# Two small row transfers in place of eight, and the last output product cut in three parts instead of four

## The chip, the cores and the metric

The kernel runs on one core of a Trainium2 chip. The metric is device time in microseconds (us) of one launch. The kernel before took 723.99 us (median of three runs, 723.14 to 724.71).

## The reference

One layer of a transformer-like block on 512 tokens of width 1024, in float32:

```
mod = silu(c) @ ada_w + ada_b;  sh1, sc1, g1, sh2, sc2, g2 = split(mod, 6)
h   = rmsnorm(x, norm1_g) * (1 + sc1) + sh1
xr, gr, u, v = split(h @ w_in, 4)
mix = concat(rg_lru(conv(xr)) * gelu(gr), spatial_gating(gelu(u), gelu(v))) @ w_out
x   = x + g1 * mix
h   = rmsnorm(x, norm2_g) * (1 + sc2) + sh2
y   = sum over each token's top-2 experts (of 32, chosen by group, then in the group):
          weight * ((silu(h @ w1[e]) * (h @ w3[e])) @ w2[e])
x   = x + g2 * y
out = rmsnorm(x, final_g)
```

All weights are read once: about 38 MB in front of the experts, 201 MB for the experts (6.3 MB each).

## The kernel before

**The front** (to about 242 us) is written out by hand in large part. SyncE issues nearly all transfers, in program order, from one queue. They use eight semaphores in turn, and a transfer is issued only when the eighth one before it has landed; a transfer into a buffer that was used before waits for the last reader as well. Transfers of 1 MB go round in five buffers (`w8`). `Ada.load` (L185 to 197) brings one unit of `ada_w` as two such buffers; `Ada.mm(kk)` (L199 to 211) is the product of one of the two halves with the condition. `Block` holds a quarter of `w_in`, split into a high and a low part by ScalarE and VectorE (L242, L244). `proj_step` (L440 to 446) is one eighth of a projection: 12 matmuls. The order on TensorE at the start is: transposes of x, `unit[0].mm(0)`, `unit[0].mm(1)`, `proj_step(b_xr, 0)`, `unit[1].mm(0)`, half of `proj_step(b_xr, 1)`, `unit[1].mm(1)`, the other half, and so on.

Between the loads of `unit[0]`, the first half of `b_xr` and those of `unit[1]`, SyncE issues the vectors that the second norm needs (norm2_g and two thirds of ada_b, L257 to 264): eight transfers into `rows_b`, each picking every fourth float of its source, so that one transpose of `rows_b` (L491) turns them, along with other vectors, into columns (`cols_b`, `cols_g`). The columns of `cols_g` are first read much later (`modulate2`).

**The experts** are worked off in 16 blocks of two or four experts, on 128 slots of tokens. Each block streams w1, w3 and w2 through a ring of twelve 1 MB buffers (`RING`, `slot8`), then computes `up(w1)`, `up(w3)`, the product with w2 (`mm`, L1161 to 1167) and adds the result to x2 by a product with a transposed one-hot matrix (`combine`).

**The last block** has four experts in column groups of 32. Its w2 product is cut by `LAST` in four parts of 256 output columns. Each part needs two buffers: a buffer holds two experts' four row chunks (two transfers of 512 KB, contiguous pieces of 1 KB). `y_part(i)` runs part i's product (four chunks q, four experts each) and scales it; all but the last are split into two parts for the combine. `combine_part(i)` adds part i to x2 for the four token tiles and sums squares on ScalarE; `scales` and `finish` apply the final norm and store. The order is y0, y1, combine 0, y2, combine 1, y3, combine 2, combine 3, then the four tiles' scaling and stores.

Of the kernel before, what the change touches and what calls it, by code (L numbers as in the profile page):

```python
# [7 lines left out]
F32 = mybir.dt.float32  # L8
# [4 lines left out]
OP = mybir.AluOpType  # L13
AX = mybir.AxisListType

P = 128
S, D, KD = 512, 1024, 8
NT = S // P
E, F, FC = 32, 512, 4
# [19 lines left out]
FIRST = ["wp"] * WP + ["wq"] * WQ + ["ft"] * 4 + ["l8"] * 3  # L39
WARM = 18  # L40
EPS = 1e-6
LAST = tuple((slice(c, c + 256), 4) for c in range(0, 1024, 256))


@with_exitstack
def trunk(ctx, tc, a, out):
    nc = tc.nc
    sync, act, pool, dve, pe = nc.sync, nc.scalar, nc.gpsimd, nc.vector, nc.tensor
# [10 lines left out]
    fa = mixer.enter_context(tc.tile_pool(name="fa", bufs=1, side="right"))  # L59
# [46 lines left out]
    off = {}  # L106
# [15 lines left out]
    rows_b = fa.tile([P, P], F32, name="rows_b")  # L122
# [11 lines left out]
    ident = const.tile([P, P], F32, name="ident")  # L134
# [30 lines left out]
    n = 0  # L165
# [88 lines left out]

    unit[0].load()
    b_xr.load(0)
    n = 40  # L257
    for name, ap in (("g2n", a["norm2_g"][0]), ("ada2", a["ada_b"][0, 3072:5120])):
        ap = ap.rearrange("(k c i) -> i k c", c=P, i=4)
        k = 4 * ap.shape[1]  # L260
        for i in range(4):
            sync.dma_start(rows_b[n + i:n + k:4], ap[i])  # L262
        off[name] = n - 40
        n += k
    unit[1].load()
    unit[2].load()
    b_xr.load(1)
# [222 lines left out]
    pt = bank("m", (P, P))  # L490
    pe.transpose(pt, rows_b, ident)  # L491
    dve.tensor_copy(cols_b, pt)
    dve.tensor_copy(cols_g, pt[:, 40:64])
    sw = [t2((P, 4, P)) for i in range(2)]
    for i in range(2):
        act.dma_start(sw[i], a["sgu_w"][0].rearrange("h i j -> i h j")[:, 4 * i:4 * i + 4, :])
# [542 lines left out]
    class Weights:  # L1039

        def __init__(self, name, b, f, cs=None, n=1):
            if b not in experts:
                experts[b] = []
                for e in range(BLOCKS[b][0], BLOCKS[b][0] + BLOCKS[b][1]):
                    if e >= FIXED:
                        e = nc.values_load(expert[0:1, e:e + 1], engines=[mybir.EngineType.SP], min_val=FIXED,
                                           max_val=E - 1)
                    experts[b].append(bass.ds(e, 1))  # L1050
            self.cs, self.f, self.n = cs, f, n
            if cs is None:
                self.src = [rows_of(a[name][0, e], f) for e in experts[b]]
            else:
                self.src = [a[name][0, e].rearrange("e (k p) f -> p (e k) f", p=P)[:, :, cs] for e in experts[b]]
            self.r = [[] for e in experts[b]]
            m = 1 if cs is None else 2
            self.todo = [(j, k) for k in range(0, self.src[0].shape[1], n) for j in range(0, len(self.src), m)]

        def load(self, most=2 * KD):  # L1060

            for q in range(min(most, len(self.todo))):
                j, k = self.todo.pop(0)
                if self.cs is None:
                    t = slot8((P, 2 * D))
                    sync.dma_start(t, self.src[j][:, k])
                    w = t.rearrange("p (i f) -> p i f", f=self.f)
                    self.r[j] += [w[:, q, :] for q in range(w.shape[1])]
                    continue
                t = slot8((P, 2, self.n, self.src[0].shape[2]))  # L1070
                for i in range(2):
                    sync.dma_start(t[:, i], self.src[j + i][:, k:k + self.n])  # L1072
                    self.r[j + i] += [t[:, i, q, :] for q in range(self.n)]

    def block_weights(b):
        if b == NB - 1:
            w2 = [Weights("expert_w2", b, D, cs, n) for cs, n in LAST]
        else:
            w2 = [Weights("expert_w2", b, D)]
        return Weights("expert_w1", b, F), Weights("expert_w3", b, F), w2  # L1080
# [9 lines left out]
    def block(b, along, early, before_y, after):  # L1090
# [67 lines left out]
                u()  # L1158
        yh, yl = yb[:, 0], yb[:, 1]

        def mm(ys, i=None):  # L1161
            for q in range(FC):
                for hf, y in enumerate(ys):
                    for c, n, j in cols:
                        w = w2[0][j][q][:, hf * F:(hf + 1) * F] if i is None else w2[i][j][q]
                        pe.matmul(y[c:c + n], gT[:, q, c:c + n], w,  # L1166
                                  start=(q == 0), stop=(q == FC - 1), tile_position=(0, c))
# [164 lines left out]
    tags = ["c", "m", "c", "m", "h"]  # L1332
    ncomb = [0]

    def y_part(i):

        cs = LAST[i][0]
        n = cs.stop - cs.start
        y = bank("y", (P, n))
        mm([y], i)  # L1340
        yf = t2((P, n))
        dve.tensor_tensor(yf, y, g2b[:, cs], op=OP.mult)
        if i == len(LAST) - 1:
            return ((cT.bitcast(F32), yf),)
        yh, yl = kept[0][:, 0, cs], kept[0][:, 1, cs]
        split(yh, yl, yf)
        return (cT, yh), (cT, yl)
# [2 lines left out]
    ms, base, both, v, r = [fin[:, n_parts - 1 + i] for i in range(5)]  # L1350

    def combine_part(i, parts):
        cs = LAST[i][0]
        n = cs.stop - cs.start
        for t in range(NT):
            ps = bank(tags[ncomb[0] % len(tags)], (P, n))
            ncomb[0] += 1
            for q, (w, y) in enumerate(parts):
                pe.matmul(ps, w[:, t, :], y, start=(q == 0), stop=(q == len(parts) - 1))
            xc = x2[:, t, cs]  # L1360
            dve.tensor_tensor(xc, xc, ps, op=OP.add)
            sq = t2((P, n))
            act.activation(sq, xc, AF.Square, scale=1.0 / 32.0, accum_out=fin[:, i, t:t + 1])
            if i < n_parts - 2:
                pool.tensor_tensor(xc, xc, fg[:, cs], op=OP.mult)
            tt = slice(t, t + 1)
            if i == n_parts - 1:
                dve.tensor_tensor(both[:, tt], base[:, tt], fin[:, i - 1, tt], op=OP.add)
                act.activation(r[:, tt], ms[:, tt], AF.Sqrt, bias=both[:, tt])
# [16 lines left out]
    todo = []  # L1386
    for i in range(n_parts):
        todo.append((i, y_part(i)))
        if 0 < i < n_parts - 1:
            combine_part(*todo.pop(0))  # L1390
    dve.scalar_tensor_tensor(base, fin[:, 0], EPS, fin[:, 1], op0=OP.add, op1=OP.add)
    for i, parts_ in todo:
        combine_part(i, parts_)
    for ts in (0, 1), (1, 3), (3, 4):
        scales(slice(*ts))
        for t in range(*ts):
# [24 lines left out]
```

## Time and profile before

| | |
|---|---|
| median of three runs | 723.99 us |
| profiled execution | 725.12 us, of which the span from the first to the last instruction is 723.3 us |
| TensorE busy | 658.3 us (91%) |
| VectorE, ScalarE, GpSimdE busy | 297.0, 178.1, 25.0 us |
| moved by DMA | 246.28 MB, mean 340 GB/s |
| mean granted TensorE clock | 0.962 |

In the profile, DMA engines are busy all the time from about 270 to 690 us (420 GB/s), and less in the front. In the rows, PE is TensorE, PEld its weight loads, DVE VectorE, ACT ScalarE, POOL GpSimdE, and SPq the issuing of transfers by SyncE. A busy share of DMA can be a little over 1 since it is worked out from packets' times.

### The profile page before, as it was taken

The page shows a single profiled execution, that of the slowest core. Times are in us where ns is not written, and L with a number is a line of the kernel's source. Part 1 is how long each engine was busy: PE and PEld are TensorE (multiplying, and loading weights), DVE is VectorE, ACT ScalarE, POOL GpSimd, SP SyncE. Part 2 cuts the span into 40 slices and gives each one's busy share as a digit, 9 for nine tenths or more (in the row PEclk, how much of TensorE's full clock was granted, in tenths as well). Part 3 has the DMA queues.
Part 4 walks back from the last instruction along what each step waited for, and adds up shares of the span by engine and source line. Part 5 has one row for each costly group of instructions (what it writes and reads, how often), then busy time and mean ns, then how long its engine had stood idle before and what let it go on. Part 6 is the DMA issues. An engine that isn't in the chain of part 4 may idle for free.

```text
span 723.3 us, 9703 instructions
## 1 busy us (share of the span) xinstructions
PE 658.3 (91%) x3693; PEld 358.2 (50%) x3693; DVE 297.0 (41%) x684; ACT 178.1 (25%) x317; POOL 25.0 (3%) x55
## 2 busy tenths in 40 slices
PE   7699999999998889987999999978799999998773
PEld 6356766777787444432444454513244445442132
DVE  7258638635468843321323333312132333224025
ACT  5135277532255121100101111000010111100114
POOL 3000001000103000000000000000000000000011
PEclk9799999999999999999999999989999999999887
DMA  8699902895528569999999999999999999999993
GB/s 295 200 346 305 318 24 97 271 367 183 218 124 316 218 255 427 400 422 420 421 423 420 420 419 422 420 421 419 423 421 420 420 422 420 421 421 421 383 335 120
DMA packets 68827, 246.28 MB, mean 340 GB/s; under 512 B 11064, under 2 KB 29096, under 8 KB 45224
## 3 DMA queue, kind: packets, MB, share of 16 engines
q1 hardware_dynamic: 67496, 245.08, 86.2%
q8 instruction: 30, 0.49, 0.3%
q10 hardware_dynamic: 1056, 0.52, 0.3%
q14 instruction: 21, 0.17, 0.1%
q0 software_dynamic: 224, 0.02, 0.0%
HBM read 243.51 MB, written 2.10 MB: 340 GB/s over the span
## 4 chain that ended last, share of the span: by engine, by line
PE 64%; DMA 21%; DVE 5%; ACT 4%; SPq 4%; issue 1%; POOL 0%; DVEq 0%; ACTq 0%
PE h L1119 21%; PE y L1166 11%; DMA w8r<-in_expert_w 10%; PE m L955 6%; DMA w<-in_expert_w 5%; PE c L969 4%; DMA l<-in_expert_w 4%; PE c L446 4%; PE h L446 3%; PE m L204 3%; PE y L446 2%; SPq L262 2%; DMA w<-in_ada_w 2%; SPq L1072 1%; PE h L90 1%
## 5 line engine op out<-in xcount | busy, mean ns | idle before, releaser
L1119 PE MATMUL h<-w,l 128*64 128x512 f32 (+1 forms) x616 | 152.5, 615 | 11.0 <-DMA w<-in_expert_w 11.0
L1119 PEld LDWEIGHTS h<-w,l 128*64 128x64 f32 (+1 forms) x616 | 42.8, 128 | 99.3 <-issue 76.6
L970 DVE TENSOR_TENSOR x<-x,c 128x512 f32<-128x512 f32 x96 | 65.8, 685 | 39.0 <-PE c L969 39.0
L1119 PE MATMUL h<-w8r,l 128*32 128x512 f32 (+1 forms) x304 | 69.8, 612 | 2.8 <-DMA w8r<-in_expert_w 2.8
L969 PE MATMUL c<-l,cT 128*128 128x512 f32 x192 | 62.6, 407 | 0.0
L1166 PE MATMUL y<-w8q,gT 128*64 128x512 f32 (+2 forms) x240 | 55.1, 626 | 5.2 <-DMA w8q<-in_expert_w 4.5
L1166 PE MATMUL y<-w8r,gT 128*64 128x512 f32 (+2 forms) x240 | 54.1, 611 | 5.5 <-DMA w8r<-in_expert_w 5.5
L955 PE MATMUL m<-l,b16h 128*128 128x256 f32 (+1 forms) x192 | 51.8, 294 | 3.1 <-ACT l L826 3.0
L994 DVE TENSOR_TENSOR t<-y,g2b 128x512 f32<-128x512 f32 x24 | 16.6, 691 | 92.3 <-PE y L1166 92.3
L1119 PE MATMUL h<-l,l 128*64 128x512 f32 (+1 forms) x120 | 52.5, 609 | 1.5 <-DMA l<-in_expert_w 1.5
L86 ACT ACTIVATE l<-t 128x512 fp32r<-128x512 f32 (+1 forms) x35 | 21.3, 612 | 128.5 <-DVE t L994 118.3
L1146 DVE SCALAR_TENSOR_TENSOR t<-t,ws,h 128x512 f32<-128x512 f32 x13 | 9.7, 747 | 97.2 <-PE h L1119 97.2
L955 PE MATMUL m<-l,b16l 128*128 128x256 f32 (+1 forms) x192 | 49.3, 281 | 0.0
L826 ACT ACTIVATE l<-m,s2c 128x256 f32<-128x256 f32 (+1 forms) x24 | 13.1, 546 | 146.2 <-PE m L955 146.2
L955 PEld LDWEIGHTS m<-l,b16h 128*128 128x128 f32 x192 | 36.3, 189 | 19.7 <-ACT l L826 8.3
L244 DVE TENSOR_TENSOR w8r<-w,w8r 128x512 fp32r<-128x512 f32 x48 | 30.6, 683 | 34.1 <-ACT w8r L242 34.1
L955 PEld LDWEIGHTS m<-l,b16l 128*128 128x128 f32 x192 | 36.3, 189 | 2.4
L1166 PEld LDWEIGHTS y<-w8r,gT 128*64 128x64 f32 (+1 forms) x240 | 15.4, 132 | 42.2 <-issue 30.0
L446 PE MATMUL c<-b16h,w8r 128*128 128x512 f32 x80 | 32.3, 427 | 4.2 <-ACT b16h L415 3.7
L242 ACT ACTIVATE w8r<-w 128x512 fp32r<-128x512 f32 x48 | 26.9, 621 | 33.1 <-PE h L92 14.1
L1119 PEld LDWEIGHTS h<-w8r,l 128*32 128x32 f32 (+1 forms) x304 | 17.8, 123 | 34.3 <-issue 28.9
L969 PEld LDWEIGHTS c<-l,cT 128*128 128x128 f32 x192 | 29.4, 189 | 6.7 <-DVE x L970 4.2
(359 smaller groups left out, 941.3 us busy)
## 6 DMA issues: line engine op xcount, KB each, us to landing
w<-in_expert_w SPq DMA_DIRECT2D x77, 1024.0 KB
w8r<-in_expert_w SPq DMA_DIRECT2D x60, 1024.0 KB
w8q<-in_expert_w SPq DMA_DIRECT2D x30, 1024.0 KB
l<-in_expert_w SPq DMA_DIRECT2D x17, 1024.0 KB
w<-in_ada_w SPq DMA_DIRECT2D x16, 1024.0 KB
w<-in_ada_w SPq DMA_DIRECT2D x16, 512.0 KB
w<-in_w_in SPq DMA_DIRECT2D x8, 1024.0 KB
w<-in_w_out SPq DMA_DIRECT2D x4, 1024.0 KB
```

Of the source, the lines that this page charges most:

```text
L86: act.activation(hi, src, AF.Copy)
L204: pe.matmul(self.ps[32 * j:32 * j + 32], cond[:, k:k + 1].to_broadcast([P, 32]), self.w[k // 4][:, j, :], start=(k < 4), stop=(k >= 4), ti ...
L242: act.activation(hi, raw, AF.Copy)
L244: return lambda: dve.tensor_tensor(lo, raw, hi.bitcast(F32), op=OP.subtract)
L262: sync.dma_start(rows_b[n + i:n + k:4], ap[i])
L446: pe.matmul(ps[c], lhs, rhs, start=(k == 0 and n == 0), stop=(k == KD - 1 and n == 2))
L955: pe.matmul(hold[k], src[:, t, chunk(k)], g[:, t, :], start=(t == 0 and i == 0), stop=(t == NT - 1 and i == 1))
L969: pe.matmul(ps, cT[:, t, :], y[:, cs], start=(i == 0), stop=(i == 1))
L970: dve.tensor_tensor(x2[:, t, cs], x2[:, t, cs], ps, op=OP.add)
L994: dve.tensor_tensor(yf, y, g2b[:, cs], op=OP.mult)
L1119: pe.matmul(h[c:c + n], xT[:, k, c:c + n], w[j][k], start=(k == 0), stop=(k == KD - 1), tile_position=(0, c))
L1166: pe.matmul(y[c:c + n], gT[:, q, c:c + n], w, start=(q == 0), stop=(q == FC - 1), tile_position=(0, c))
```

## The change

The second norm's vectors come as two transfers of whole rows into a small tile `rows_d` (six rows of 512 floats). Four transposes, each taking every fourth column of `rows_d`, make the columns, and one copy puts them in the same order as before into `cols_g`.

`LAST` is now one part of 512 columns and two of 256. A buffer holds the same row chunks of all four experts: one chunk for the half, two for a quarter. It is filled by four transfers of 256 KB (pieces of 2 KB for the half, of 1 KB for the quarters). `y_part` may be given something to run between its chunks 0 to 1 and 2 to 3: combine 0 stands amid the second part's product, combine 1 amid the third's; combine 2 ends the work.

```diff
-LAST = tuple((slice(c, c + 256), 4) for c in range(0, 1024, 256))
+LAST = (slice(0, 512), slice(512, 768), slice(768, 1024))
...
-    for name, ap in (("g2n", a["norm2_g"][0]), ("ada2", a["ada_b"][0, 3072:5120])):
-        ap = ap.rearrange("(k c i) -> i k c", c=P, i=4)
-        k = 4 * ap.shape[1]
-        for i in range(4):
-            sync.dma_start(rows_b[n + i:n + k:4], ap[i])
+    rows_d = fa.tile([6, 512], F32, name="rows_d")
+    sync.dma_start(rows_d[0:2], a["norm2_g"][0].rearrange("(k f) -> k f", f=512))
+    sync.dma_start(rows_d[2:6], a["ada_b"][0, 3072:5120].rearrange("(k f) -> k f", f=512))
...
-    dve.tensor_copy(cols_g, pt[:, 40:64])
+    pt = bank("m", (P, 4, 6))
+    for i in range(4):
+        pe.transpose(pt[:, i, :], rows_d.rearrange("r (c i) -> r i c", i=4)[:, i, :], ident[0:6, 0:6])
+    dve.tensor_copy(cols_g.rearrange("p (r i) -> p i r", i=4), pt)
...
+            self.n = n = 1 if cs is None else 2048 // (len(self.src) * (cs.stop - cs.start))
+            self.todo = [(j, k) for k in range(0, self.src[0].shape[1], n)
+                         for j in range(len(self.src) if cs is None else 1)]
...
-                t = slot8((P, 2, self.n, self.src[0].shape[2]))
-                for i in range(2):
-                    sync.dma_start(t[:, i], self.src[j + i][:, k:k + self.n])
+                t = slot8((P, len(self.src), self.n, self.src[0].shape[2]))
+                for j, s in enumerate(self.src):
+                    sync.dma_start(t[:, j], s[:, k:k + self.n])
...
+            mm([y], i, range(FC // 2))
+            between()
+            mm([y], i, range(FC // 2, FC))
...
+    part0 = y_part(0)
+    part1 = y_part(1, lambda: combine_part(0, part0))
+    def second_part():
+        combine_part(1, part1)
+        dve.tensor_scalar(base, fin[:, 0], EPS, None, op0=OP.add)
+    combine_part(2, y_part(2, second_part))
```

SyncE's queue at the start, as a piece of the difference (- before, + after); `w_155` is the first half of `b_xr`, `w_165` and `w_160` the first buffer of `unit[1]`:

```order
 L234 DMA w_155<-in_w_in 128x4x512
-L262 DMA rows_b<-in_norm_g 2x128x1 x4
-L262 DMA rows_b<-in_ada_b 4x128x1 x4
-L194 DMA w_165<-in_ada_w 128x4x256 x2
-L194 DMA w_168<-in_ada_w 128x4x256 x2
-L194 DMA w_171<-in_ada_w 128x4x256 x2
+L258 DMA rows_d<-in_norm_g 2x512
+L259 DMA rows_d<-in_ada_b 4x512
+L194 DMA w_160<-in_ada_w 128x4x256 x2
+L194 DMA w_163<-in_ada_w 128x4x256 x2
+L194 DMA w_166<-in_ada_w 128x4x256 x2
```

Two transfers stand now where eight stood, ahead of the same loads of `unit[1]`.

TensorE at the end of the program, before; y is the w2 product (L1166), `cT` the one-hot matrix of the combine, `t_5329` the last part's scaled result:

```order
L1166 MATMUL y<-w8r,gT 32x256 x16
L1359 MATMUL m<-l_2120,cT 128x256 x2
L1359 MATMUL h<-l_2120,cT 128x256 x2
L1359 MATMUL c<-l_2120,cT 128x256 x2
L1359 MATMUL m<-l_2120,cT 128x256 x2
L1359 MATMUL c<-t_5329,cT 128x256
L1359 MATMUL m<-t_5329,cT 128x256
L1359 MATMUL h<-t_5329,cT 128x256
L1359 MATMUL c<-t_5329,cT 128x256
```

Here all 16 matmuls of y's last part run first, and then the combines of the last two parts.

The same place after; the last part's result is `t_5321`:

```order
L1166 MATMUL y<-w8r,gT 32x256 x8
L1364 MATMUL h<-l_2120,cT 128x256 x2
L1364 MATMUL c<-l_2120,cT 128x256 x2
L1364 MATMUL m<-l_2120,cT 128x256 x2
L1364 MATMUL c<-l_2120,cT 128x256 x2
L1166 MATMUL y<-w8r,gT 32x256 x8
L1364 MATMUL m<-t_5321,cT 128x256
L1364 MATMUL h<-t_5321,cT 128x256
L1364 MATMUL c<-t_5321,cT 128x256
L1364 MATMUL m<-t_5321,cT 128x256
```

The eight matmuls of the last but one combine moved ahead of the last eight matmuls of y, and y's last part is cut in two groups of eight.

SyncE's last weight transfers after, with what each waits for (`DMAHW` is one of the eight semaphores of landed transfers; `w8_5046` and `w8_5051` are buffers of the half):

```order
L1072 DMA w8_5046<-in_expert_w2 128x512 [waits DMAHW6_49,PE_49]
L1072 ISA
L1072 DMA w8_5046<-in_expert_w2 128x512 [waits DMAHW7_49]
L1072 ISA
L1072 DMA w8_5046<-in_expert_w2 128x512 [waits DMAHW0_49]
L1072 ISA
L1072 DMA w8_5046<-in_expert_w2 128x512 [waits DMAHW1_49]
L1072 ISA
L1072 DMA w8_5051<-in_expert_w2 128x512 [waits DMAHW2_49,PE_49]
```

Each transfer is now half as large (the last block's w2 comes in 32 instead of 16), and there are still eight semaphores.

## Rows read from the trace of the kernel before

**Rows 1.** The page's clock and DMA lines, in 40 slices, in tenths

```profile
PEclk9799999999999999999999999989999999999887
DMA  8699902895528569999999999999999999999993
```

**Rows 2.** Chain of waits from 0 to 110 us: start, us, what

```profile
9.51 1.32 SPq L262
10.87 6.66 SPq L262
...
23.84 0.94 SPq L194
...
25.92 8.37 DMA w<-in_ada_w
34.34 1.11 PE m L204 x8
...
39.58 0.23 PE h L446
```

**Rows 3.** Windows of 2 us: busy by engine, clock, DMA share, GB/s

```profile
22.00:24.00 2.00, 2.00 (x6) 1.51 (x6) 1.11 (x2) 0.00 (x0) 0.00 (x0) 0.50 0.25 2
...
26.00:28.00 2.00, 0.19 (x1) 0.00 (x0) 0.00 (x0) 0.00 (x0) 0.00 (x0) 0.94 1.01 345
...
40.00:42.00 2.00, 2.00 (x8) 0.70 (x10) 1.48 (x3) 0.00 (x0) 0.00 (x0) 0.50 1.08 360
42.00:44.00 2.00, 2.00 (x16) 0.36 (x8) 0.00 (x0) 0.00 (x0) 0.00 (x0) 0.67 1.10 348
```

**Rows 4.** Timeline, TensorE around 26 us: start, us, instruction [idle before]

```profile
25.56 0.63 PE L446 MATMUL c<-b16l,w8r 128*128 128x512 f32 x1
29.65 1.94 PE L204 MATMUL m<-w,cond 128*32 128x512 f32 x8 [3.46 <-DMA w<-in_ada_w]
```

**Rows 5.** Chain of waits from 676 us on

```profile
687.00 8.40 DMA l<-in_expert_w
...
698.85 8.90 DMA w8r<-in_expert_w
...
707.79 1.93 PE y L1166 x26
...
717.70 0.72 ACT x L1381
```

**Rows 6.** Timeline, small operations like those that are added

```profile
2.26 0.24 PE L340 MATMUL m<-ident,rows_c 8*128 8x8 f32 x1 [2.26 <-DMA rows_c<-in_c]
3.45 0.32 SPq L114 DMA_DIRECT2D rows_a<-in_ada_b  x1
51.08 0.49 PE L446 MATMUL c<-b16h,w8r 128*128 128x512 f32 x1 [0.47 <-DVE w8r L244]
```

**Rows 7.** Chain of waits from 110 to 310 us

```profile
119.06 1.29 DVE w8r L244 x2
120.37 5.33 DMA w<-in_ada_w
...
307.46 15.05 DMA w<-in_expert_w
```

**Rows 8.** Timeline of the last block and the end

```profile
683.89 0.13 PEld L1119 LDWEIGHTS h<-w,l 128*32 128x32 f32 x1 [2.42 <-DMA w<-in_expert_w]
...
710.69 0.60 PE L1359 MATMUL c<-t,cT 128*128 128x256 f32 x2
...
712.31 0.40 ACT L1363 ACTIVATE t<-x 128x256 f32<-128x256 f32 x1
```

**Rows 9.** Windows of 10 and 2 us with different transfer shapes

```profile
140.00:150.00 10.00, 10.00 (x48) 7.95 (x50) 2.50 (x4) 2.20 (x4) 0.00 (x0) 1.00 1.04 384
...
698.00:700.00 2.00, 1.11 (x10) 0.49 (x8) 1.69 (x5) 1.18 (x6) 0.31 (x1) 1.00 1.10 350
...
718.00:720.00 2.00, 0.00 (x0) 0.00 (x0) 0.39 (x1) 0.42 (x1) 0.00 (x0) 0.50 1.02 380
```

More of the change, by code (lines that the diff above doesn't have):

```diff
@@ L256, in trunk @@
     b_xr.load(0)
-    n = 40
-    for name, ap in (("g2n", a["norm2_g"][0]), ("ada2", a["ada_b"][0, 3072:5120])):
-        ap = ap.rearrange("(k c i) -> i k c", c=P, i=4)
-        k = 4 * ap.shape[1]
-        for i in range(4):
-            sync.dma_start(rows_b[n + i:n + k:4], ap[i])
-        off[name] = n - 40
-        n += k
+    rows_d = fa.tile([6, 512], F32, name="rows_d")
+    sync.dma_start(rows_d[0:2], a["norm2_g"][0].rearrange("(k f) -> k f", f=512))
+    sync.dma_start(rows_d[2:6], a["ada_b"][0, 3072:5120].rearrange("(k f) -> k f", f=512))
+    off["g2n"], off["ada2"] = 0, 8
     unit[1].load()
@@ L1039, in trunk, with __init__ @@
     class Weights:
-        def __init__(self, name, b, f, cs=None, n=1):
+        def __init__(self, name, b, f, cs=None):
             if b not in experts:
@@ L1050, in __init__ @@
                     experts[b].append(bass.ds(e, 1))
-            self.cs, self.f, self.n = cs, f, n
+            self.cs, self.f = cs, f
             if cs is None:
@@ L1056, in __init__ @@
             self.r = [[] for e in experts[b]]
-            m = 1 if cs is None else 2
-            self.todo = [(j, k) for k in range(0, self.src[0].shape[1], n) for j in range(0, len(self.src), m)]
+            self.n = n = 1 if cs is None else 2048 // (len(self.src) * (cs.stop - cs.start))
+            self.todo = [(j, k) for k in range(0, self.src[0].shape[1], n)
+                         for j in range(len(self.src) if cs is None else 1)]
         def load(self, most=2 * KD):
@@ L1069, in load @@
                     continue
-                t = slot8((P, 2, self.n, self.src[0].shape[2]))
-                for i in range(2):
-                    sync.dma_start(t[:, i], self.src[j + i][:, k:k + self.n])
-                    self.r[j + i] += [t[:, i, q, :] for q in range(self.n)]
+                t = slot8((P, len(self.src), self.n, self.src[0].shape[2]))
+                for j, s in enumerate(self.src):
+                    sync.dma_start(t[:, j], s[:, k:k + self.n])
+                    self.r[j] += [t[:, j, q, :] for q in range(self.n)]
     def block_weights(b):
         if b == NB - 1:
-            w2 = [Weights("expert_w2", b, D, cs, n) for cs, n in LAST]
+            w2 = [Weights("expert_w2", b, D, cs) for cs in LAST]
         else:
@@ L1159, in block, with mm @@
         yh, yl = yb[:, 0], yb[:, 1]
-        def mm(ys, i=None):
-            for q in range(FC):
+        def mm(ys, i=None, qs=range(FC)):
+            for q in qs:
                 for hf, y in enumerate(ys):
@@ L1333, in trunk, with y_part @@
     ncomb = [0]
-    def y_part(i):
-        cs = LAST[i][0]
+    def y_part(i, between=None):
+        cs = LAST[i]
         n = cs.stop - cs.start
         y = bank("y", (P, n))
-        mm([y], i)
+        if between is None:
+            mm([y], i)
+        else:
+            mm([y], i, range(FC // 2))
+            between()
+            mm([y], i, range(FC // 2, FC))
         yf = t2((P, n))
@@ L1352, in combine_part @@
     def combine_part(i, parts):
-        cs = LAST[i][0]
+        cs = LAST[i]
         n = cs.stop - cs.start
@@ L1363, in combine_part @@
             act.activation(sq, xc, AF.Square, scale=1.0 / 32.0, accum_out=fin[:, i, t:t + 1])
-            if i < n_parts - 2:
+            if i == 0:
                 pool.tensor_tensor(xc, xc, fg[:, cs], op=OP.mult)
@@ L1384, in finish @@
             sync.dma_start(o[:, t, hf * 512:(hf + 1) * 512], x2[:, t, hf * 512:(hf + 1) * 512])
[L1386 to L1393, printed above, removed]
+    part0 = y_part(0)
[4 more added lines that the diff above has]
+    combine_part(2, y_part(2, second_part))
     for ts in (0, 1), (1, 3), (3, 4):
```

## Prediction, written before the changed kernel was run

> **What bounds the kernel now.** I read the page first. Its DMA line says 9 from about 270 us on, so the experts are bound by the stream of weights; ahead of that the digits go down to 0, so the front is not [rows 1]. What the front gains therefore reaches the end only if the stream starts earlier too. Then I read the chain of waits of the front, for what holds it at each place. The reader is to see a long piece there: from 9.51 to 23.84 us the chain is nothing but SyncE issuing L262, the eight element-wise transfers, and only then come the loads of `unit[1]`, which TensorE is waiting for [rows 2]. The windows say the same from the other side: at 22 to 24 us DMA moves 2 GB/s, at 26 to 28 us 345 GB/s [rows 3]. So the weights are late because their issue is late, not because the memory is slow. Next the timeline of TensorE: it ends `proj_step(b_xr, 0)` at 25.56 + 0.63 = 26.19 us, idles 3.46 us on `w<-in_ada_w`, runs `unit[1].mm(0)` at 29.65 and `unit[1].mm(1)` at 34.34 [rows 2, 4]. Last I read the chain of the last block: landing weights, the product with the last ones, the vector work, the store [rows 5].
>
> **The front, step by step.** Removed: 23.84 - 9.51 = 14.3 us of SyncE's queue. Added: two transfers of a few whole rows. The nearest row is the one of 48 rows in rows_a, 0.32 us to issue [rows 6], so 0.65 us. The loads of `unit[1]` can thus be issued from about 10.3 us on. That is not all gain, for the engines still carry x, `unit[0]` and `b_xr` then; the second L262 took 6.66 us [rows 2], perhaps for that reason. If SyncE is held until the end of that piece (17.53 us) whatever it issues, the loads are still 23.84 - 17.53 = 6.3 us earlier, and the two products could start at 29.65 - 6.3 = 23.4 and 34.34 - 6.3 = 28.0 us. TensorE isn't free before 26.19. So the next that is late is TensorE itself, in either case, and the gain is counted there and not on the queue:
>
> - `unit[1].mm(0)` starts at 26.2. [...] Without the idle stretch I take the higher level, about 1.0 us.
> - Six matmuls of `proj_step(b_xr, 1)`, 0.23 us each [rows 2]: 1.4 us.
> - `unit[1].mm(1)` then starts at 26.2 + 1.0 + 1.4 = 28.6 in place of 34.34 us: 5.7 us earlier. All that follows hangs on it.
>
> Both ends: at the lower level the same two steps take 1.9 and 2.6 us, the start is 30.7, the gain 3.6 us. On the other side, before has a half-speed stretch from 40 to some 43.3 us (0.50, then 0.67 on average [rows 3]), which costs about 1.7 us; if the changed timing keeps the clock up there, the gain is 7.4. I take 5.7, since the activity just ahead of 26 us is the same as before.
>
> The four transposes: a matmul of that kind shows 0.24 us with its latency [rows 6], four are at most 1.0 us. They stand behind the transpose of rows_b, and shortly after it TensorE waits 0.47 us on VectorE's split (L244) [rows 6]; I count 0 and keep 0.5 us as the end of the range, should that cover be gone. The copy from them replaces a copy. The queue of SyncE has no other step moved; ScalarE and VectorE keep their order in the front.
>
> Does the gain last to the experts? From 39 to 242 us the chain is TensorE with ScalarE and VectorE, each waiting on the other. The one transfer in it that lasts (5.33 us at 120.37) follows directly on VectorE's split at 119.06 that frees its buffer, so it moves along [rows 7]. The stream of experts enters the chain at 307.46 us, after TensorE's release of a buffer [rows 7], and moves with it too. I carry all of 5.7 us through.
>
> **The end, step by step.** The frame is that of before.
>
> - The stream. The last of w3 lands at 683.84 (TensorE stops waiting at 683.89 [rows 8]), the first half of w2 at 687.00 + 8.40 = 695.40 [rows 5]: 4.19 MB in 11.6 us, in pieces of 1 KB. Pieces of 2 KB moved 384 GB/s in 140 to 150 us, those of 1 KB 350 GB/s in 698 to 700 [rows 9]. With 384 the half takes 10.9 us: 0.65 us gained. With 350 it takes 12.0, a loss of 0.4. The quarters keep their 1 KB pieces and the 12.35 us to the last landing at 707.75 [rows 5]. Last landing: 707.1.
> - The product behind it. In before the last part's 16 matmuls (1.93 us) nearly all wait for the last landing, since each chunk needs all four experts and the last buffer holds two of them [rows 5]. After, the last buffer holds chunks 2 and 3, half of the work: 0.97 us, so 0.96 gained. The product ends at 708.1 instead of 709.72.
> - The combine. In before the third part's combine and its squares stand between; the last part's first product starts at 710.69 and its first square at 712.31, which is 2.6 us after the end of the product [rows 8]. After: a product of 0.60, a scaling and an addition of about 0.4 each (by the square of the same size, 0.40 [rows 8]) and gaps make 1.6 us. 1.0 us gained. The third part's combine is hidden in the wait for the last buffer (3 us a buffer), if TensorE keeps up: it needs about 2 us of these three.
> - Unchanged: four squares, roots and scalings, the stores. They move as one piece, from the first square to ScalarE's last instruction at 717.70 [rows 5].
>
> Together 0.65 + 0.96 + 1.0 = 2.6 us. [...]
>
> **Sum.** 5.7 + 2.6 = 8.3 us off the profiled execution of 725.12 us: 716.8. The profiled execution is 1.13 us above the median of 723.99, so I expect 715.7 us.
>
> **Rivals.** [...]
>
> Second, the clock stays up at 40 us as well: 7.4 + 2.6 = 10.0, hence 714.0 us.
>
> Third, slower: the smaller transfers starve the stream. Only eight may be under way, now 8 x 0.262 = 2.1 MB instead of 4.2. If one takes as long from issue to landing as before (8.40 and 8.90 us [rows 5]), the stream carries 2.1 MB in 8.65 us, 242 GB/s; w2's 8.39 MB take 34.6 us instead of 23.9, 10.7 us more. Against 5.7 of the front and 2.0 of the product and combine that is 2.7 us slower: 726.7 us. It decides from about 7.8 us to landing on. Against it: the 8.4 us hold some five transfers of 1.5 us queued ahead (0.52 MB at 350 GB/s). After the idle stretch the first two transfers, issued from 23.84 on, were in use at 29.65 [rows 2, 4]: 5.8 us, of which 3.0 are moving 1.05 MB, so 2.8 us without a queue. With 0.75 us for its own bytes a transfer needs 3.6 us, and five under way suffice. Also, the eight stores of 256 KB ran at 380 GB/s together [rows 9].
> [...]
>
> Fourth, it doesn't do what it says: the 5.7 us are given back before the experts, for instance at a wait for a buffer that the trace of before hides. [...] Against it: no transfer in the chain from 39 to 300 us but the one named.
>
> **Chances and range.** My forecast 0.50, first rival 0.27, second 0.14, third 0.04, fourth 0.05. The range goes from the second rival with a faster half (380 GB/s and more, at most 1.6 us more) to the first with both places slow: 712.4 to 719.9 us. 0.2% of 724 is 1.45 us, about what a measurement can tell from no change. Only the third rival is slower; of the fourth, half lies within 0.2%. Faster 0.93, same 0.03, slower 0.04.
>
> **What would show it.** Right, if SyncE issues the loads of `unit[1]` before 18 us, `unit[1].mm(1)` runs at about 28.6 us, the first expert product (242 us before) starts 5 to 6 us earlier, and from the last landing to the last ScalarE instruction it is about 8.7 us instead of 10.7. Wrong, if a DMA wait appears at 26 us, if the front's shift shrinks between 39 and 242 us, or if the windows of the last 25 us of weights show less than 330 GB/s.

## The result and the profile after

The changed kernel took 715.28 us (median of four runs, 713.19 to 718.51) against 724.35 us for the kernel before, measured beside it: a ratio of 0.9875, 95% interval 0.9836 to 0.9913. Forecast were 715.7 us. The profiled execution of after took 718.51 us, the longest of its four, with a span of 716.6 us; that of before took 725.12. So the two traces differ by 6.6 us and the medians by 9.1, and the terms below are read from the traces.

**The front.** The chain of waits of after (start, us, what) answers to [rows 2]:

```profile
10.06 9.93 DMA w<-in_w_in
...
26.30 0.99 PE m L204 x8
...
28.88 1.04 PE m L204 x8
...
35.88 3.18 PE m L204 x16
```

The long piece of SPq is gone, and so is the DMA wait at 26 us: `unit[1].mm(0)` follows directly on `proj_step(b_xr, 0)`, and `unit[1].mm(1)` runs at 28.88 us in place of 34.34. SyncE's queue shows why:

```profile
10.47 0.36 SPq L258 DMA_DIRECT2D rows_d<-in_norm_g  x1
10.88 1.13 SPq L259 DMA_DIRECT2D rows_d<-in_ada_b  x1
12.05 12.55 SPq L194 DMA_DIRECT2D w<-in_ada_w  x8
```

The loads of `unit[1]` begin to be issued at 12.05 us; before it was 23.84. The windows of 2 us (the columns of [rows 3]) show weights moving where 2 GB/s moved before, and TensorE's clock:

```profile
22.00:24.00 2.00, 2.00 (x5) 1.61 (x6) 1.93 (x4) 0.57 (x1) 0.00 (x0) 0.50 1.10 350
24.00:26.00 2.00, 2.00 (x8) 1.51 (x7) 0.36 (x1) 0.00 (x0) 0.00 (x0) 0.78 1.10 347
26.00:28.00 2.00, 2.00 (x13) 0.83 (x12) 0.00 (x0) 0.00 (x0) 0.00 (x0) 1.00 1.10 349
...
36.00:38.00 2.00, 2.00 (x12) 0.40 (x9) 0.00 (x0) 0.00 (x0) 0.00 (x0) 0.50 1.11 342
```

At 26 to 28 us the granted clock is 1.00, the higher level, as the forecast took it; the half-speed stretch of 40 us in before is now at 36 (0.50), where sixteen matmuls take 3.18 us.

**Amid the experts.** The first expert product and TensorE's last wait for w3 in the last block, after:

```profile
236.94 7.51 PE L1119 MATMUL h<-w,l 128*64 128x512 f32 x33
...
679.79 0.13 PEld L1119 LDWEIGHTS h<-w,l 128*32 128x32 f32 x1 [2.36 <-DMA w<-in_expert_w]
```

and the first expert product before:

```profile
242.41 7.51 PE L1119 MATMUL h<-w,l 128*64 128x512 f32 x33
```

The product starts 5.47 us earlier. But the last wait for w3 ends at 679.79 us, before at 683.89 [rows 8]: 4.10 us earlier. Of the 1.37 us between, 1.24 are lost at one place, the w2 product of the first block, which no row of mine had shown. TensorE's timeline there, after:

```profile
258.79 1.07 PE L1166 MATMUL y<-w8q,gT 128*64 128x512 f32 x3 [0.69 <-ACT gT L984]
261.13 3.17 PE L1166 MATMUL y<-w8q,gT 128*64 128x512 f32 x13 [1.27 <-issue]
263.76 3.97 PE L1166 MATMUL y<-w8r,gT 128*64 128x512 f32 x16
```

and before:

```profile
264.27 3.90 PE L1166 MATMUL y<-w8q,gT 128*64 128x512 f32 x16 [0.69 <-ACT gT L985]
268.00 3.60 PE L1166 MATMUL y<-w8r,gT 128*64 128x512 f32 x16
```

After, TensorE stops for 1.27 us behind three matmul records (a record is one matmul as the trace lists it), and the profile names no cause ("issue"). From the product's first half to its second it takes 4.97 us, before 3.73.

**The end.** The chain of waits of after, answering to [rows 5]:

```profile
687.71 6.04 DMA w8q<-in_expert_w
693.77 6.00 DMA w8r<-in_expert_w
699.81 1.05 PE y L1166 x10
...
702.66 1.06 PE y L1166 x10
...
711.27 0.72 ACT x L1386
```

The product behind the last landing takes 1.06 us (before 1.93). From w3's last wait (679.79) to the last landing, at which the product goes on (702.66), it is 22.87 us; before 23.90 (683.89 to 707.79 [rows 5, 8]). From the product's end (703.72) to the start of ScalarE's last instruction it is 7.55 us; before 7.98 (709.72 to 717.70).

### The profile page after: what moved, and what is told of

It is laid out like the page before. It is cut to its first block, busy times and chain, and to the rows that moved or that the text cites. A ratio compares the mean times of both kernels' runs of the same rounds, so it can differ in the third digit from the quotient of the medians.

```text
span 716.6 us, 9650 instructions
## 1 busy us (share of the span) xinstructions
PE 658.0 (92%) x3657; PEld 357.2 (50%) x3657; DVE 297.4 (42%) x678; ACT 177.3 (25%) x308; POOL 24.6 (3%) x51
## 4 chain that ended last, share of the span: by engine, by line
PE 52%; DMA 37%; DVE 5%; ACT 4%; issue 1%; SPq 1%; POOL 0%; DVEq 0%; ACTq 0%
PE h L1119 14%; DMA w<-in_expert_w 11%; DMA l<-in_expert_w 11%; DMA w8r<-in_expert_w 11%; PE y L1166 7%; PE c L442 4%; PE m L954 4%; PE h L442 3%; PE c L968 3%; PE m L204 3%; PE y L442 3%; DMA w<-in_w_in 1%; PE h L90 1%; DMA x<-in_x 1%; PE h L91 1%
## 5 line engine op out<-in xcount | busy, mean ns | idle before, releaser
L1119 PE MATMUL h<-w,l 128*64 128x512 f32 (+1 forms) x616 | 155.4, 622 | 11.7 <-DMA w<-in_expert_w 11.7
L1119 PE MATMUL h<-w8r,l 128*32 128x512 f32 (+1 forms) x304 | 73.2, 630 | 2.8 <-DMA w8r<-in_expert_w 2.8
L1166 PE MATMUL y<-w8r,gT 128*64 128x512 f32 (+2 forms) x240 | 54.7, 601 | 5.3 <-DMA w8r<-in_expert_w 5.0
L1166 PE MATMUL y<-w8q,gT 128*64 128x512 f32 (+2 forms) x240 | 54.2, 601 | 5.6 <-DMA w8q<-in_expert_w 3.5
L1166 PEld LDWEIGHTS y<-w8r,gT 128*64 128x64 f32 (+1 forms) x240 | 16.0, 131 | 41.5 <-issue 29.0
```

The source lines that it names most:

```text
L1119: pe.matmul(h[c:c + n], xT[:, k, c:c + n], w[j][k], start=(k == 0), stop=(k == KD - 1), tile_position=(0, c))
L1166: pe.matmul(y[c:c + n], gT[:, q, c:c + n], w, start=(q == 0), stop=(q == FC - 1), tile_position=(0, c))
```

## The experiments

Twelve kernels ran. Times are medians, ratios are to runs of before on the same chip (medians 723.99, 724.25 and 724.47 us in the three sets) and can differ a little from the ratio of the two medians, and "tail" is the time from w3's last wait to the last landing.

**e1_front: the first edit alone.**

```diff
-        for i in range(4):
-            sync.dma_start(rows_b[n + i:n + k:4], ap[i])
...
+    sync.dma_start(rows_d[0:2], a["norm2_g"][0].rearrange("(k f) -> k f", f=512))
+    sync.dma_start(rows_d[2:6], a["ada_b"][0, 3072:5120].rearrange("(k f) -> k f", f=512))
```

> The kernel before with the first edit alone (two row transfers, four transposes); the end is that of before. My theory: the front's gain is the start of unit[1]'s second product, 5.5 us earlier (28.9 for 34.34 us in the profiles), and it passes through the experts whole: about 5.5 us less than before, 718.5 us, first expert product at 237 us, from the last landing to the last ScalarE instruction as before, 10.7 us. Rival: part of it is given back among the experts (2 us were lost there between the profiles of before and of the change): 3.5 us less, 720.5 us. Rival that the end makes most of the gain: 2 us less or nothing.

719.03 us (717.72 to 720.64), ratio 0.9944 (0.9926 to 0.9963): 5.0 us gained by the medians, 2.7 to 5.4 by the interval of the ratio. That lies between the 5.5 us of the theory and the 3.5 of its first rival, and the time does not part the two; the front is the larger part of the gain. First expert product at 233.89 us, tail 24.01 us, product's end to last ScalarE instruction 7.98: the end is that of before.

**e2_tail: the second edit alone.**

```diff
-LAST = tuple((slice(c, c + 256), 4) for c in range(0, 1024, 256))
+LAST = (slice(0, 512), slice(512, 768), slice(768, 1024))
```

> The kernel before with the second edit alone (half and two quarters, all experts in a load, combines amid the products); the front is that of before. My theory: from w3's last landing to ScalarE's last instruction 30.9 us as in the profile of the change, against 33.8, so 2.9 us less than before, about 721.3 us; first expert product at 242.5 us. Rival, the eight semaphores starve the stream of w2: no gain or a loss, 724 us or more. Rival that the clock decides the end: the time from the last landing to the last instruction is 10 us or more.

721.0 us (719.2 to 723.0), ratio 0.996 (0.9945 to 0.9975): 3.0 us. First expert product at 241.46, tail 22.15 us. By the medians, and within their scatter, the two edits add up: 5.0 + 3.0 = 8.0 us, against 8.7 for both (723.99 - 715.28) or 9.1 by the pair of medians above.

**e3_pool: before, the eight element-wise transfers from GpSimdE's queue.**

```diff
-            sync.dma_start(rows_b[n + i:n + k:4], ap[i])
+            pool.dma_start(rows_b[n + i:n + k:4], ap[i])
```

> The kernel before, with the eight element-wise transfers issued from GpSimdE's queue behind its other row transfers in place of SyncE's; they move the same 3072 single floats and everything else stays. My theory: what they cost is their place in SyncE's queue, so the loads of unit[1] are issued before 18 us, unit[1]'s second product starts at about 28.9 us and the time is that of the first edit alone, 5.5 us below before. Rival: the single floats load the DMA engines themselves, so unit[1]'s weights come late anyway: unit[1]'s second product at 31 us or later, gain under 3 us.

728.9 us (727.6 to 729.74), ratio 1.0073 (1.0055 to 1.0091): slower by 4.9 us. My theory fell. SyncE's queue was free, and the first half of `b_xr` landed 19.54 us after its issue at 9.85 us, where after the change it took 9.93. `unit[1].mm(1)` (here L212) ran at 38.40 us, not at 28.9. Both in the chain, and two windows of 2 us:

```profile
9.85 19.54 DMA w<-in_w_in
...
38.40 1.04 PE m L212 x8
```

```profile
14.00:16.00 2.00, 0.48 (x8) 0.19 (x8) 1.25 (x3) 0.00 (x0) 1.84 (x3) 1.00 1.25 99
20.00:22.00 2.00, 0.00 (x0) 0.00 (x0) 0.00 (x0) 0.00 (x0) 0.00 (x0) 0.68 1.45 102
```

DMA engines are busy (share 1.25 and 1.45) and move 99 and 102 GB/s, where the same windows of after have 379 and 351. So from GpSimdE's queue the 3072 single floats are work for the DMA engines themselves, and what runs beside them is slowed. In SyncE's queue little ran beside them: in before 2 GB/s moved at 22 to 24 us [rows 3]. Packets of under 512 bytes number 11064 in before and 7974 in e1_front: 3090 fewer, for 3072 floats.

**e4_512k: the change, the half in eight transfers of 512 KB in place of sixteen of 256 KB** (`m` is 2 experts in a buffer for the half, 4 for the quarters).

```diff
-                t = slot8((P, len(self.src), self.n, self.src[0].shape[2]))
-                for j, s in enumerate(self.src):
-                    sync.dma_start(t[:, j], s[:, k:k + self.n])
+                t = slot8((P, self.m, self.n, self.src[0].shape[2]))
+                for i in range(self.m):
+                    sync.dma_start(t[:, i], self.src[j + i][:, k:k + self.n])
```

> The kernel after the change, with the half's weights in eight transfers of 512 KB (two experts and two row chunks in a buffer, pieces of 2 KB) in place of sixteen of 256 KB; the quarters stay. Theory of the eight semaphores: in the change's profile the half's stream fell to 311 to 343 GB/s because SyncE may have only 2.1 MB under way; here it moves at 380 and more, and the last landing is about 1.0 us earlier counted from w3's last landing (21.3 for 22.3 us). Rival, the stream is limited by the pieces or by what is loaded beside: the same 22.3 us, the same time as the change, 715.3 us.

715.57 us (713.82 to 717.74), ratio 0.9895 (0.9875 to 0.9915), tail 22.82 us against 22.87 in after: the same as the change. So here the eight semaphores do not bound the stream with 256 KB a transfer.

**e5_floats_late: before, the element-wise transfers behind the loads of `unit[1]`, still on SyncE.**

```diff
+    unit[1].load()
     for name, ap in (("g2n", a["norm2_g"][0]), ("ada2", a["ada_b"][0, 3072:5120])):
...
-    unit[1].load()
```

> The kernel before, with its eight element-wise transfers (3072 single floats) moved in SyncE's queue behind the loads of unit[1]; nothing else is changed. Theory, as it stands after the run from GpSimdE's queue: the floats cost what stands behind them, wherever they are. unit[1].mm(1) then runs at about 28 to 29 us as after the change, but unit[2] and the second half of b_xr are issued some 14 us later, so the chain waits for them at about 36 us: of the 5.5 us, 0 to 5 are left at the first expert product (237 to 242 us), and the time lies between 719 and 724 us. Rival, only the place ahead of unit[1] cost: the first expert product at about 237 us and 719 us, as with the front alone. Third, the floats take bandwidth from the loads beside them, as from GpSimdE's queue: later than before, above 724 us.

723.12 us (720.91 to 725.57), ratio 0.9988 (0.9974 to 1.0002): no difference that can be told. TensorE's timeline:

```profile
27.77 1.06 PE L204 MATMUL m<-w,cond 128*32 128x512 f32 x8
35.94 1.06 PE L204 MATMUL m<-w,cond 128*32 128x512 f32 x8 [1.38 <-DMA w<-in_ada_w]
40.03 1.94 PE L204 MATMUL m<-w,cond 128*32 128x512 f32 x8 [3.02 <-DMA w<-in_ada_w]
```

`unit[1].mm(1)` at 27.77 as after the change, and then two new waits for `unit[2]`; the first expert product is at 240.56 us. The theory holds: in SyncE's queue the floats hold up what comes next, here `unit[2]` (waits of 1.38 and 3.02 us), and moving them there only moves the wait.

**e6_six_rows: the first edit alone, each row a transfer of its own** (one run).

```diff
-    sync.dma_start(rows_d[0:2], a["norm2_g"][0].rearrange("(k f) -> k f", f=512))
+    for i in range(2):
+        sync.dma_start(rows_d[i:i + 1], a["norm2_g"][0].rearrange("(k f) -> k f", f=512)[i:i + 1])
```

> The first edit alone, but the six rows of norm2_g and ada_b in six transfers of one row each in place of two. Theory: it is the single floats that cost, not the number of transfers; six times 0.3 to 0.4 us of issue, unit[1]'s loads about 1.5 us later, hidden, unit[1].mm(1) at about 28 us and the time near 719 us. Rival: a small transfer costs its place in the queue of eight semaphores, near the 1.3 us or more of each element-wise one; unit[1]'s loads are 6 us or more later than with two, and a wait for DMA appears at 26 us.

719.76 us. In SyncE's queue:

```profile
10.36 0.69 SPq L259 DMA_DIRECT2D rows_d<-in_norm_g  x2
11.10 3.94 SPq L261 DMA_DIRECT2D rows_d<-in_ada_b  x4
16.32 10.51 SPq L194 DMA_DIRECT2D w<-in_ada_w  x8
```

The first two take 0.35 us each, the next four about 1 us each, so `unit[1]`'s loads start 4.3 us later than after; still no DMA wait appears at 27 us. On the time the theory is right (719.0 for two transfers), on the price of issue the truth lies between the two.

**e7_warm: the change, with unread matmuls in two idle stretches of the front**, six behind the first modulate of `unit[0]`, four behind the second of `unit[1]`.

```diff
+    keep_warm(6)
...
+    keep_warm(4)
```

> The change, with matmuls whose result nobody reads (six behind the first modulate of unit[0], four behind the second of unit[1]) put where TensorE waits at about 19 to 22 and 32 to 35 us. [...] Rival: the clock falls anyway, or the added work itself delays the chain: 715 us or more.

715.93 us (712.65 to 716.92), ratio 0.9881 (0.986 to 0.9903): no gain in time against after, as the rival has it. Yet the windows from 14 to 40 us all show a granted clock of 1.00, and the first expert product comes at 233.51 us. It is lost again at the first block's w2 product, where a larger stop stands than after, this time ahead of the first record, and the granted clock from 255 to 260 us is 0.69:

```profile
257.30 5.13 PE L1168 MATMUL y<-w8q,gT 128*64 128x512 f32 x16 [2.62 <-PEq L1285]
262.25 3.62 PE L1168 MATMUL y<-w8r,gT 128*64 128x512 f32 x16
```

The line named, L1285, is `with tc.If(n > 0)`: TensorE jumps there over code for tokens beyond the blocks' slots, which isn't needed in this data, straight to this product. That gave a new theory: the code behind the jump isn't there yet.

**e8_not_amid: the change, combines behind the next part's product and not amid it.**

```diff
-    part1 = y_part(1, lambda: combine_part(0, part0))
+    part1 = y_part(1)
+    combine_part(0, part0)
...
+    part2 = y_part(2)
+    combine_part(1, part1)
```

> The change, but the combines of the first and the second part run behind the next part's whole product and not between its second and third chunk; the cut in three parts and the loads stay. Theory: the order of the combines is worth at most about 1 us (the first square 1.75 us after the last product's end in the profile after would come at about 2.6 us, as before), so the time is 715 to 716.5 us, and most of the end's 3 us comes from the loads (the last landing 22.3 us after w3's last instead of 23.9, and half the product behind it). Rival: the combines amid the products are what the end's gain comes from: 718 us.

717.53 us (716.85 to 718.04), ratio 0.9912 (0.9896 to 0.9928). Product's end to the last ScalarE instruction is 8.09 us (702.01 to 710.10), against 7.55: the order is worth 0.54 us in the trace. The medians differ by 2 us, and the intervals of the two ratios overlap. Tail 22.86 us. The trace stands with the theory; the time is above the theory's 715 to 716.5 us and nearer to the rival's 718, and what the other 1.5 us are, I can't say.

**e9_fewer: the change, with the same unread matmul time at the start in fewer instructions**: 18 matmuls (36 records) become 9 (18 records).

```diff
-    keep_warm(WARM)
+    keep_warm(6)
+    pt = bank("m", (P, 512))
+    for i in range(3):
+        pe.matmul(pt.rearrange("p (o c) -> p o c", o=4), ident,
+                  ident.rearrange("p (o c) -> p o c", o=1).to_broadcast([P, 4, P]), start=True, stop=True)
```

> The change, with twelve of the eighteen matmuls of the first keep_warm (128 columns) replaced by three of 512 columns: the same TensorE time, 18 matmul records fewer ahead of the first block. Theory: in the runs with the new front TensorE stops after three records of block 0's w2 product, right behind a jump over code that isn't needed (0.57 to 1.27 us that no engine causes, 1.2 to 1.9 us lost in all), since its next piece of code arrives late; the four added transposes put the piece's border there, and before it lay after eight records. With 18 records fewer it lies at about the 21st, the first 16 records take 3.65 us as in the best case, and the time is 1.2 to 1.6 us less than the change: about 714. Rival: the stop comes from the transfers of that moment (the front is early), and stays: 715.3, and a stop of 0.6 us or more.

714.36 us (711.77 to 715.28), ratio 0.9861 (0.9839 to 0.9883). The stop is gone:

```profile
257.69 3.65 PE L1170 MATMUL y<-w8q,gT 128*64 128x512 f32 x16 [0.69 <-ACT gT L988]
261.18 3.61 PE L1170 MATMUL y<-w8r,gT 128*64 128x512 f32 x16
```

First half to second half 3.49 us. In time the gain of 0.9 us is too small to be told apart from the change; the trace shows it.

**e10_warm_fewer: e7's matmuls, and still fewer instructions at the start** (two of 128 columns, four of 512; 12 records).

```diff
-    keep_warm(WARM)
+    keep_warm(2)
+    for i in range(4):
...
+    keep_warm(6)
+    keep_warm(4)
```

> The change with both: unread matmuls in the two idle stretches of the front that keep the clock up, and sixteen of the eighteen first ones replaced by four of 512 columns. Theory: the stretches filled gave a first expert product at 233.5 us, but their twenty records put the border of the code ahead of the product, where 2.62 us were lost; without that loss, block 0's w2 product (its first 16 records) takes 3.65 us and the time is 712 to 713 us. Rival: what the front gains is lost again later in any case: 715 to 716 us.

712.67 us (711.68 to 713.47), ratio 0.9837 (0.9819 to 0.9855): the lowest median of all. It is faster than before beyond doubt; its interval still overlaps with that of the change (0.9836 to 0.9913), so that it beats the change is likely and not settled. `unit[1].mm(1)` at 26.63 us, the first expert product at 233.11, and nearly no stop:

```profile
254.96 4.19 PE L1172 MATMUL y<-w8q,gT 128*64 128x512 f32 x16 [0.69 <-ACT gT L990]
258.62 3.97 PE L1172 MATMUL y<-w8r,gT 128*64 128x512 f32 x16
```

```profile
22.00:24.00 2.00, 2.00 (x10) 1.38 (x8) 1.46 (x3) 0.00 (x0) 0.00 (x0) 1.00 1.10 351
...
36.00:38.00 2.00, 2.00 (x14) 1.82 (x13) 0.32 (x3) 0.00 (x0) 0.00 (x0) 1.00 1.10 346
```

The granted clock is 1.00 in both windows in which after has 0.50. That the unread matmuls keep it up is likely and not proven. With them both profiles show 1.00 at 22 to 24 us (e7, e10). Of the seven with this front and without them, after, e1 and e4 show 0.50 there, and in e6, e8 and e9 the matmuls come 0.43 us apart as in after; but in e12 they come 0.23 us apart without any help, as in e7 and e10.

**e11_four_more: before, with four matmul records more at the start.**

```diff
-    keep_warm(WARM)
+    keep_warm(WARM - 2)
+    for i in range(4):
+        pe.matmul(pt[:, 0:64], ident, ident[:, 0:64], start=True, stop=True)
```

> The kernel before, with two of the first eighteen unread matmuls cut into four of 64 columns: the same TensorE time and four records more, as many as the change's four transposes. Theory: the border of the code moves from eight to about three records into block 0's w2 product; its first 16 records take about 5.0 us in place of 3.9, and the time is about 1.1 us more than before. Rival: no stop without the early front; 3.6 to 4.2 us and 724 us.

725.09 us (722.51 to 727.07), ratio 1.001 (0.9996 to 1.0025): no difference in time. In the trace the stop appears with the old front, behind the fourth record, but smaller than expected:

```profile
264.67 1.08 PE L1169 MATMUL y<-w8q,gT 128*64 128x512 f32 x4 [0.69 <-ACT gT L988]
266.24 2.80 PE L1169 MATMUL y<-w8q,gT 128*64 128x512 f32 x12 [0.50 <-issue]
268.87 3.60 PE L1169 MATMUL y<-w8r,gT 128*64 128x512 f32 x16
```

4.20 us from half to half, 0.47 more than before; 1.1 were expected.

**e12_quarters: the change, four quarters in place of a half and two quarters.**

```diff
-LAST = (slice(0, 512), slice(512, 768), slice(768, 1024))
+LAST = tuple(slice(c, c + 256) for c in range(0, 1024, 256))
```

> The change with four quarters in place of a half and two quarters; loads of all four experts, transfers of 256 KB and the combines amid the next part's products stay. So the pieces of the first half are 1 KB long and not 2 KB. Theory: the stream's gain (22.3 us from w3's last landing to the last one, before 23.9) comes from the half's longer pieces: about 23.1 to 23.9 us here, and 0.7 to 1.5 us more than the change. Rival: it comes from the smaller transfers of all four experts, whatever the pieces: 22.3 us and the same time as the change.

716.72 us (713.3 to 718.03), ratio 0.9903 (0.9886 to 0.992): 1.4 us above the change, as the theory wants, but the two intervals overlap. Tail 23.79 us, in the range of the kernels with the old end and just above that of the kernels with a half (see below). Windows of the stream in this kernel, pieces of 1 KB:

```profile
680.00:682.00 2.00, 1.31 (x20) 0.82 (x24) 0.00 (x0) 0.60 (x1) 0.00 (x0) 1.00 1.07 351
682.00:684.00 2.00, 2.00 (x40) 0.93 (x32) 0.42 (x1) 0.32 (x1) 0.00 (x0) 1.00 1.08 341
```

and of e4_512k, pieces of 2 KB:

```profile
678.00:680.00 2.00, 1.09 (x7) 0.18 (x3) 0.75 (x1) 0.00 (x0) 0.00 (x0) 1.00 1.06 388
680.00:682.00 2.00, 1.31 (x12) 0.62 (x16) 0.00 (x0) 0.60 (x1) 0.00 (x0) 1.00 1.05 386
```

These windows alone don't settle it, since after's own windows of the half (678 to 688 us, pieces of 2 KB) show 311 to 383 GB/s. The landings of the single transfers, taken from the semaphore updates in the traces, do. In six of the seven kernels with a half, e4 apart, its transfers of 256 KB land 0.65 us apart (median, 403 GB/s) and those of the quarters behind it, also of 256 KB but in pieces of 1 KB, 0.75 us apart (350 GB/s). Transfers of 512 KB land 1.35 us apart in pieces of 2 KB (e4) and 1.5 us apart in pieces of 1 KB (the old end). In e12 the first sixteen land 0.72 us apart. In these landings the piece decides, with transfers of 256 KB and of 512 KB alike, and the theory holds.

## Why the prediction was right, point by point

**The front, 5.7 us forecast, 5.47 measured.** Where the next limit lies was right: TensorE at the end of `proj_step(b_xr, 0)`, at the higher clock. `unit[1].mm(1)` came at 28.88 us, 28.6 forecast. The 1.0 us taken for `unit[1].mm(0)` stands in no row of before; in after it takes 0.99 us, at a granted clock of 1.00. The matmuls of `proj_step` come 0.43 us apart where the granted clock is 0.50 (before, 24.28 to 25.56 us), so that six take the 2.6 us of the lower level, and 0.23 us apart where it is 1.00 (after, 27.56 to 28.48 us). The four transposes take 0.57 us in the chain:

```profile
44.43 0.57 PE m L491 x4
```

That the size fits so well is in part luck. `proj_step(b_xr, 0)` began 1.22 us later than in before (21.92 and 20.70 us) and ended at nearly the same time (26.30 and 26.19 us) only because the clock rose within it: its last five records take 0.39 to 0.40 us, in before 0.63. And the profiled execution of after is one of several: in six profiles with this front (after, e1, e4, e8, e9, e12) the first expert product comes at 231.9 to 236.9 us, on average 234.8, so against before's 242.41 the gain there is 5.5 to 10.5 us, and 5.47 is the least of them. Three of the six (e1, e4, e12) are the fastest or second fastest execution of their kernel, after's is the slowest of its four.

One sentence was half wrong: that the weights were late "because their issue is late, not because the memory is slow". e3 shows that the floats also slow the transfers beside them, so taking them from SyncE's queue without making rows of them would have cost 4.9 us. e5 shows the other half: behind `unit[1]` they are as dear as ahead of it.

**"I carry all of 5.7 us through": the step that failed.** In the profile 4.10 us arrive at the last w3, and 1.24 of the lost 1.37 go at the first block's w2 product. It is the fourth rival in small: a wait that the rows of before did not show. From the product's first half to its second half, by the place of the stop:

| matmul records ahead of the stop | runs | us |
|---|---|---|
| none seen (21 by count, 3 + 18) | e9 | 3.49 |
| none seen (8 by count, as in before) | e2 | 3.49 |
| 8 | before | 3.73 |
| 7 (in e10 also by count, 3 + 24 - 20) | e3, e5, e10 | 3.63, 3.48, 3.66 |
| 4 | e11 | 4.20 |
| 3 | after, e1, e4, e6, e8, e12 | 4.97, 4.55, 4.28, 4.60, 4.48, 4.30 |
| 3 - 20 by count, so ahead of the product | e7 | 4.95, and 2.62 idle ahead of it in place of 0.69 |

The place follows the number of instructions that stand ahead of it in TensorE's program, with an early front and a late one (e9 and e11). In before the chain breaks behind eight records, with 0.02 us between the pieces:

```profile
264.27 1.94 PE y L1166 x8
266.23 5.37 PE y L1166 x24
```

e11 has four records more, and the stop is behind four. The change has four transposes more, and it is behind three. The six runs with the stop at three take 4.53 us on average, e2, before, e3, e5 and e10 3.60. So by this table the four transposes, counted at nothing, cost about 0.9 us, some 215 us later, by their number and not by their time. The profile counts 30 packets and 0.49 MB for an instruction queue, 16 KB each.

The single packets of that queue, in the traces, fit the theory that the code behind the jump isn't there yet. Between one packet and the next TensorE runs mostly 100 to 150 matmul records and as many weight loads; only between those at 258.70 and 264.51 us of after, around the product, 19. In every kernel but after and e7 a packet starts 0.03 to 0.09 us behind TensorE's last matmul ahead of the jump, and in after 0.60 us behind it. It takes 0.92 to 1.20 us. In the eleven kernels where TensorE stops within the product, it goes on 1.26 to 1.53 us behind the packet's end, wherever the stop is: 1.52 in after, 1.43 in before, 1.27 in e11, 1.34 in e10. This would also tell why after, with the latest packet, has the longest stop of its row. That TensorE waits for what the packet brings is inferred from these times; what starts the packet, and why it was late in after, the traces don't show.

**The stream, 0.65 us forecast, 1.03 measured.** The tail of the six kernels with the old end is 23.4 to 24.3 us (mean 23.97), of the seven with a half 22.15 to 23.65 (mean 22.93); e12 without the 2 KB pieces has 23.79. The term was right in its cause, and about 0.4 us too small. By the landings the gain lies in the half, as forecast: from w3's last wait it takes 10.3 us in after (10.9 forecast) and 11.5 in before, on average 10.8 in the seven and 11.7 in the six; the quarters behind it take 12.15 and 12.23 on average. In e12 the first half takes 12.2. The window criterion was too strict: single windows of after at 311 and 290 GB/s stand in a tail that is shorter all the same, and before itself has two of 310 and 301 (684 to 688 us).

**The product behind the last landing, 0.96 forecast, 0.87 measured.** As worked out: half the matmuls wait.

**The combine, 1.0 us forecast, 0.43 measured.** I measured to the first square, and that did come 0.84 us earlier (1.75 us behind the product, before 2.59 [rows 8]). The step that failed is that the rest moves "as one piece, from the first square to ScalarE's last instruction": between the starts of these two lie 5.80 us after and 5.39 before. The end hangs on VectorE. After, its four additions follow TensorE's products, and only then the first scaling:

```profile
704.97 0.42 DVE L1366 TENSOR_TENSOR x<-x,m 128x256 f32<-128x256 f32 x1 [0.79 <-PE m L1364]
...
706.26 0.42 DVE L1366 TENSOR_TENSOR x<-x,m 128x256 f32<-128x256 f32 x1
...
706.67 0.15 DVE L1378 TENSOR_TENSOR fin<-fin 128x1 f32<-128x1 f32 x1
```

The first scaling starts 2.95 us behind the product, before 3.39 (713.11). The third part's additions, which were removed from this stretch, had been done in before while VectorE would have waited for TensorE. From the last landing to the end of ScalarE's work it is 9.3 us (702.66 to 711.99), not the 8.7 named.

**The rivals.** The third, a starved stream, falls by after and by e4: from w3's last wait to the last landing it was 22.87 us in after and 22.82 in e4, and twice the bytes under way change nothing. Its price was added up wrongly (10.7 less 5.7 and 2.0 is 3.0 us and 727.0, not 2.7 and 726.7), which changes no verdict. The first rival of the chances, a lower granted clock in the front or at the end, and the second, a higher one at 40 us, are no matter of the code alone: at 32 to 39 us the same sixteen matmuls take 1.92 us in e1, e4, e8 and e12 (granted clock 1.00 at 36 to 38 us in e1 and e4), but 3.25 in after (0.50) and 3.56 in e9. So the second rival came true in some executions, and it is part of the scatter of the first expert product, 231.9 to 236.9 us in six profiles with the change's front (after, e1, e4, e8, e9, e12). e10, with a granted clock of 1.00 at 22 to 28 and at 36 to 38 us, has 233.11 and times from 711.68 to 713.47. The slow end of the range, 719.9 us, takes both places at the lower clock; no run shows the terms of that sum, and the longest execution of after took 718.51 us.

Terms with opposite errors (the front's loss of 1.4, the combine's 0.6; the stream's 0.4) and a profiled run of after that lies 3.2 us above its median make the sum in the profile 6.6 us instead of 8.3; the medians give 9.1. That the median comes within 0.4 us of the forecast is therefore in part luck.

## What to carry to other kernels

Eight transfers of single floats kept the next loads from SyncE's queue until 23.84 us, where two of whole rows kept them until 12.05, and from GpSimdE's queue they slowed the transfers beside them (99 GB/s in place of 379, e3); load whole rows and turn them on chip, and don't look for another queue for the floats. Behind a jump in a long program count the instructions ahead of it as well as their time: here four more of them went with a stop far behind them (1.27 us in after, 0.50 in e11), and with wider matmuls that do the same work it was gone (e9). Where a vector chain ends a kernel, follow the engine whose instructions stand in order (here VectorE), not the first one that starts earlier: the first square came 0.84 us earlier, the end only 0.43.

## What the runs showed of the hardware that was not expected

- Beside eight transfers of 3072 floats in all DMA moved 99 and 102 GB/s in two windows, at a busy share of 1.25 and 1.45 (e3), where after has 379 and 351.
- A stop of 0.5 to 1.3 us in TensorE behind a jump, 2.62 where the product itself had not begun (e7), with a place that moves with the number of instructions ahead; where it stops within the product, TensorE goes on 1.26 to 1.53 us behind the end of a 16 KB packet of the instruction queue.
- Transfers of 256 KB and of 512 KB, eight under way, gave the same time (715.28 and 715.57 us), while transfers in pieces of 1 KB landed at about 350 GB/s (0.75 us apart for 256 KB) and those in pieces of 2 KB at 388 to 403 (0.65 us apart for 256 KB).
- With unread matmuls in TensorE's idle stretches (2.69 us ahead of 21.92 us in after) the granted clock was 1.00 at 22 to 24 us (e7, e10), where it was 0.50 in after, e1 and e4.
